# Seven-product MLP kernel: factor splits in two groups, two input sums and all input differences placed amid the first down projection

## The chip, the cores and the metric

One Trainium2 chip, one of its cores. The metric is the device time of one execution in microseconds (us); lower is better. Before the change three runs took 1106.09, 1107.44 and 1108.67 us, median 1107.44 us. Engines are named as in the profile: PE (TensorE matmul, its weight loads PEld), DVE (VectorE), ACT (ScalarE), POOL (GpSimd), SP (SyncE).

## The reference, cut to what matters

A step of a two-layer encoder for 512 prompt tokens and 64 tokens of a running stream (576 columns in all, D = 1024). Layer 0 mixes by pooling, layer 1 by sparse attention; each is followed by the same MLP with a hidden width of 4096:

```python
def _mlp(h, w_up, w_down):
    u = jax.nn.relu(h @ w_up)
    return (u * u) @ w_down
...
        x = x + y.astype(x.dtype)
        x = x + _mlp(_rmsnorm(x, norm_mlp[i]), mlp_w_up[i], mlp_w_down[i]).astype(x.dtype)
```

The change touches only the two MLPs.

## The kernel before, in words

**Layout.** Activations stand transposed: x[k] is a tile of 128 features by 576 tokens, k = 0..7. A float32 product is made of three passes of a reduced type (fp32r): each operand is split into a high part (ACT casts it) and a low part (DVE subtracts the high part from the operand), and the passes are high x high, high x low and low x high. Weight blocks go through the same split in `split_unit` (L182 on ACT makes `wh`, L183 on DVE makes `wl`). Six such units are held at a time, so a weight cast on ACT waits until PE has finished with the unit six places earlier, and DVE's low part waits for the cast.

**Seven products.** `mlp` works in four chunks of 1024 hidden columns. Apart from the up projection of chunk 0 (the plain up: 8 blocks of 48 matmuls in `project`, L306), all is done by `seven` (L497): two by two blocks (two output blocks by the two token halves of 288) are made by seven products instead of eight, 84 matmuls where the plain way takes 96. The price is sums of the inputs. A pair of hidden blocks needs seven factors: b11, b22, b21 as they are and the sums t1, t2, t3, t4. After the plain up `finished` makes them: DVE takes ReLU and scale out of PSUM (L464), ACT squares (L456), DVE forms the sums (`first_sum`, `middle_sums`, `last_sum`, L477 to L484), and `parts_of` splits the factors into `u` (ACT cast L473, DVE subtraction L474). For the first two and the third pair it splits all seven factors in one instruction on each engine, 2016 columns wide. There is one buffer `v` for the unsplit factors of a pair, so that the next pair's L464 waits for the subtraction that reads the last of `v`.

**Sums of x.** The up projections of chunks 1 to 3 are made by `seven` too and need the same of their input: for each of four pairs (x[j], x[j+4]) `x_sums(j)` makes t1, t2, t4 (one ACT activation, three DVE instructions L432 to L434, an ACT cast L435, a DVE subtraction L436), and `x_difference(j)` makes t3 in the place of a quarter of the split input `xs[j]` (DVE L441 and L442, ACT cast L443, DVE L444). The difference overwrites what the plain up reads, so it has to come behind the plain up's matmuls; `x_sums` reads x itself, so it has to come ahead of the down projection that updates those blocks of x in place. Before the change the program has `x_sums(0)` and `x_sums(1)` between the plain ups, `x_sums(2)`, `x_sums(3)` and all four differences at their end, then the four down projections of chunk 0.

**Down.** `Down(q)` with `seven` makes the output blocks x[2q] and x[2q+1]: seven products over the four pairs of the chunk, and six DVE updates of x out of PSUM (L555), some of which must be done before PE may go on in that bank.

**Order.** DMAs are issued by SP (weights) and POOL (sums of weight blocks by accumulating DMA) in the order of a list `jobs`. The order of instructions on each engine is set when the program is built, by a scheduler; it may move an instruction ahead of its place in the code. Each engine then runs its own list strictly in order. Names such as `u_1050` carry a buffer number of the built program; they differ between the two programs.

Of the kernel before, what the change touches and what calls it, by code (L numbers as in the profile page):

```python
# [46 lines left out]
SPARE_UNITS = 6  # L47
RAWS = (4, 3)
MLP_BLOCKS = ("up", "even", "odd", "down")
PLAIN_CHUNKS = 1  # L50
SEEDED = 4
LEAD = 5
UP_ORDER = (0, 4, 1, 5, 2, 6, 3, 7)
FACTORS = ("t3", "t1", "t2", "b11", "b22", "b21", "t4")


@with_exitstack
def pool_dsa_kernel(ctx: ExitStack, tc: tile.TileContext, a, o):
# [13 lines left out]
    def uid(s):  # L72
        count[0] += 1
        return f"{s}_{count[0]}"
# [76 lines left out]
    def mlp_jobs(layer, plain=0):  # L151
        for c in range(4):
            for n, f in enumerate(UP_ORDER):
                kind = "up" if c < PLAIN_CHUNKS else "odd" if n % 2 else "even"
# [127 lines left out]
    def next_block(sub=dve):  # L282
        return [next_unit(5 - i, sub) for i in range(2)]
# [114 lines left out]
    def mlp(layer, gi, late=0, end=None):  # L398
# [22 lines left out]
        def pairs(c):  # L421

            return (KT - LAST if end and c == 3 else KT) // 2

        def x_sums(j):

            t = x_sums_tile()
            xt.append(t)
            raw, first = rough[:, 3 * j:3 * j + 3], rough[:, 12 + j % 2]
            gain, minus = gv[:, gi, j:j + 1], negative[:, half + j:half + j + 1]  # L430
            act.activation(first, x[j][:, :HT], AF.Copy, scale=gain)
            dve.scalar_tensor_tensor(raw[:, 0], x[j][:, HT:], gain, first, ALU.mult, ALU.subtract)  # L432
            dve.scalar_tensor_tensor(raw[:, 1], x[half + j][:, :HT], minus, raw[:, 0], ALU.mult, ALU.subtract)
            dve.scalar_tensor_tensor(raw[:, 2], x[half + j][:, HT:], minus, raw[:, 1], ALU.mult, ALU.subtract)  # L434
            act.copy(t[:, :, 0], raw)  # L435
            dve.tensor_tensor(t[:, :, 1], raw, f32(t[:, :, 0]), ALU.subtract)  # L436

        def x_difference(j):

            b12, b22 = xs[j][:, :, :HT], xs[half + j][:, :, :HT]  # L440
            dve.tensor_tensor(snap, f32(b22), f32(b12), ALU.subtract)  # L441
            dve.tensor_tensor(snap[:, 0], snap[:, 0], snap[:, 1], ALU.add)  # L442
            act.copy(b12[:, 0], snap[:, 0])  # L443
            dve.tensor_tensor(b12[:, 1], snap[:, 0], f32(b12[:, 0]), ALU.subtract)  # L444
# [13 lines left out]
        def activated(pt, v):  # L458

            if isinstance(pt, tuple):  # L460
                for h in range(2):
                    dve.scalar_tensor_tensor(v[:, h], pt[h][:, :HT], 0.0, halves(norm.rb)[:, h], ALU.max, ALU.mult)
            else:
                dve.scalar_tensor_tensor(v, pt[:, :, :HT], 0.0, halves(norm.rb), ALU.max, ALU.mult)  # L464
            square(v)

        def tiles():
            return (phase["acts"].tile([P, 7, HT], F32, tag="v", bufs=1, name=uid("v")),
                    phase["u"].tile([P, 7, 2, HT], F32R, tag="u", bufs=4, name=uid("u")))

        def parts_of(u, v, f):

            act.copy(u[:, f, 0], v[:, f])  # L473
            dve.tensor_tensor(u[:, f, 1], v[:, f], f32(u[:, f, 0]), ALU.subtract)  # L474

        def first_sum(v):
            dve.tensor_tensor(v[:, 1], v[:, 3], v[:, 0], ALU.subtract)  # L477

        def middle_sums(v):
            dve.scalar_tensor_tensor(v[:, 2], v[:, 4], -1.0, v[:, 1], ALU.mult, ALU.subtract)  # L480
            dve.tensor_tensor(v[:, 0], v[:, 4], v[:, 0], ALU.subtract)

        def last_sum(v):
            dve.scalar_tensor_tensor(v[:, 6], v[:, 5], -1.0, v[:, 2], ALU.mult, ALU.subtract)  # L484
# [94 lines left out]
        class Up:  # L579
# [15 lines left out]
                act.copy(snap[:, 1], self.banks[1])  # L595

            def lo0(self):
                self.relu(3, self.banks[0], ALU.max, 1)
                ahead()
                if self.final:  # L600
                    parts_of(self.u, self.v, slice(3, 4))

            def hi1(self):
                v = self.v
                dve.tensor_tensor(v[:, 4], self.banks[1], snap[:, 0], ALU.add)  # L605
                self.relu(4, v[:, 4], ALU.min, 0)
                ahead()

            def hi0(self):
                v = self.v  # L610
                dve.tensor_tensor(v[:, 0], self.banks[2], snap[:, 1], ALU.add)
                self.relu(0, v[:, 0], ALU.max, 0)
                if end and self.at[0] == 3:
                    left_over(self.at[1], v[:, 0])
                parts_of(self.u, v, slice(4 if self.final else 3, 5))
                first_sum(v)
                middle_sums(v)

            def lo1(self):
                v = self.v  # L620
                self.relu(5, self.banks[1], ALU.min, 1)
                if not self.final:
                    ahead()
                parts_of(self.u, v, slice(0, 3))
                last_sum(v)
                if not self.final:
                    ahead()
                parts_of(self.u, v, slice(5, 7))
# [12 lines left out]
        def finished(i, pt, us):  # L641
            nonlocal pair
            if i % 2 == 0:
                pair = tiles()
            v, u = pair
            activated(pt, v[:, 4:6] if i % 2 else v[:, 0:4:3])
            if i == KT - 2:
                first_sum(v)
                for f in (3, 1):
                    parts_of(u, v, slice(f, f + 1))  # L650
            elif i == KT - 1:
                middle_sums(v)
                last_sum(v)
                parts_of(u, v, slice(0, 3, 2))
                parts_of(u, v, slice(4, 7))
# [8 lines left out]
        todo = []  # L664
        snap = None
        for c in range(4):
            us = []
            if c < PLAIN_CHUNKS:
                for i in range(KT):
                    w = next_block()  # L670
                    spreads = c == 0 and i == 2
                    pt = (psum1("up"), psum1("up")) if spreads else psum("up")
                    project(pt, w, xs, spread() if spreads else iter(()))
                    todo.append((i, pt, us))
                    if c == 0 and i < 2:
                        if i:
                            norm.stats()
                        continue
                    for t in todo:
                        finished(*t)  # L680
                    todo.clear()
                    if c == 0 and 3 <= i < 7 and i % 2:
                        x_sums(i // 2 - 1)
# [7 lines left out]
            else:  # L691
                for j in range(half):
                    up = Up(c, j)
                    seven(of_x, False, up)
                    us.append(up.u)
            for q in range(pairs(c)):
                seven(of(us), q == 0, Down(q))
        if end:
            rest = []
            for j in range(half):  # L700
# [857 lines left out]
```

## Time and profile before

| what | value |
|---|---|
| runs shown | 1106.09, 1107.44, 1108.67 us |
| the profiled execution | 1105.9 us, its span 1104.1 us |
| PE busy | 1058.5 us (96%), 7942 matmul records |
| DVE busy | 910.8 us (82%) |
| ACT busy | 628.7 us (57%) |
| granted PE clock, mean | 0.985 |
| plain up of layer 0 / layer 1 | 41 to 96 us / 700 to 755 us |
| down projections of chunk 0 in layer 0 | from 96 us; the first copy of the next up projection (L592) is at 154.7 us |

Times in a row of the timeline are microseconds from the span's start: start, duration, engine, line, operation, output <- input, shape, count, and in brackets the engine's idle time before it and what ended it. PE is busy nearly all the time, so the places where it waits are what can be won. "PEclk" is the share of full clock that PE was granted.

### The profile page before, as it was taken

To read this page: it belongs to the slowest core of one execution; us is meant where nothing else is said; L and a number is where in the kernel's file an instruction comes from. 1 tells how busy PE (TensorE), PEld (TensorE's weight loads), DVE (VectorE), ACT (ScalarE), POOL (GpSimd) and SP (SyncE) were. 2 spreads that over 40 slices of the span, in tenths; PEclk is the share of its full clock that TensorE was granted. 3 is DMA by queue.
4 is the path that set the end of the run, shared out by engine and by line. 5 is a ranking of instruction groups with operands and counts; after the bars stand their busy time and mean duration, and the time that the engine had idled before them with its cause. 6 is when DMAs were issued, how large, how long until landed. Compare 5 with 4: busy or idle time off the path is not lost.

```text
span 1104.1 us, 21662 instructions
## 1 busy us (share of the span) xinstructions
PE 1058.5 (96%) x7942; PEld 1030.0 (93%) x7942; DVE 910.8 (82%) x1837; ACT 628.7 (57%) x1232; POOL 263.4 (24%) x285
## 2 busy tenths in 40 slices
PE   9997999999999999999989999997999999999996
PEld 8997999999999998999979888997999999999895
DVE  7779779879978977779998935679789879978973
ACT  8555357546646745454378776455456547547641
POOL 4100111111111100217687892000111111111101
PEclk9998999999999999999999999998999999999998
DMA  8332666666576564456642454442666676676512
GB/s 248 92 98 74 139 166 164 153 167 160 154 174 163 150 186 134 125 170 173 198 111 66 131 176 117 143 96 67 152 157 164 162 166 162 157 164 163 126 56 86
DMA packets 94459, 157.66 MB, mean 143 GB/s; under 512 B 13729, under 2 KB 25296, under 8 KB 94352
## 3 DMA queue, kind: packets, MB, share of 16 engines
q1 hardware_dynamic: 68720, 109.80, 32.3%
q0 software_dynamic: 15840, 28.84, 16.7%
q10 hardware_dynamic: 9792, 17.63, 5.1%
q8 instruction: 62, 1.02, 0.4%
q14 instruction: 45, 0.37, 0.1%
HBM read 141.15 MB, written 10.89 MB: 138 GB/s over the span
## 4 chain that ended last, share of the span: by engine, by line
PE 80%; DVE 9%; ACT 4%; POOL 2%; issue 2%; DMA 1%; SPq 0%; DVEq 0%; ACTq 0%; POOLq 0%
PE b L497 28%; PE c L497 14%; PE up L306 8%; PE pj L306 7%; PE a L497 7%; PE wo L306 3%; DVE wl L183 2%; PE sc L1255 2%; PE wa L306 1%; PE v L1155 1%; PE pt L1281 1%; PE pb L989 1%; PE dn L306 1%; DVE u L474 1%; ACT wh L182 1%
## 5 line engine op out<-in xcount | busy, mean ns | idle before, releaser
L182 ACT CAST wh<-raw 128x512 fp32r<-128x512 f32 (+1 forms) x316 | 195.3, 620 | 241.2 <-PE b L497 86.1
L183 DVE TENSOR_TENSOR wl<-raw,wh 128x512 fp32r<-128x512 f32 (+1 forms) x294 | 207.7, 708 | 35.8 <-ACT wh L182 29.6
L497 PE MATMUL b<-u,wh 128*128 128x288 f32 x992 | 206.1, 300 | 16.0 <-DVE u L474 6.7
L497 PEld LDWEIGHTS b<-u,wh 128*128 128x128 f32 x992 | 161.5, 191 | 19.9 <-DVE u L474 7.8
L182 ACT CAST wh<-sum 128x512 fp32r<-128x512 f32 x165 | 101.7, 620 | 86.8 <-PE b L497 47.7
L497 PE MATMUL b<-u,wl 128*128 128x288 f32 x496 | 146.8, 298 | 0.0
L183 DVE TENSOR_TENSOR wl<-sum,wh 128x512 fp32r<-128x512 f32 x165 | 112.3, 690 | 34.9 <-ACT wh L182 32.7
L239 POOL DMA_DIRECT2D sum<-in_w_down x31 | 27.1, 891 | 338.0 <-DVE u L474 125.2
L497 PE MATMUL c<-u,wh 128*128 128x288 f32 x496 | 104.5, 298 | 0.1
L497 PEld LDWEIGHTS b<-u,wl 128*128 128x128 f32 x496 | 94.2, 191 | 0.0
L306 PE MATMUL up<-xs,wh 128*128 128x288 f32 x512 | 89.2, 296 | 1.0 <-DVE v L464 1.0
L474 DVE TENSOR_TENSOR u<-v,u 128x576 fp32r<-128x576 f32 (+3 forms) x92 | 81.0, 888 | 6.2 <-ACT u L473 6.2
L497 PE MATMUL b<-xt,wh 128*128 128x288 f32 x384 | 78.1, 296 | 6.8 <-DVE v L605 6.8
L497 PEld LDWEIGHTS c<-u,wh 128*128 128x128 f32 x496 | 80.7, 189 | 1.4 <-DVE x L555 1.2
L497 PE MATMUL b<-xs,wh 128*128 128x288 f32 x384 | 77.2, 295 | 0.0
L306 PEld LDWEIGHTS up<-xs,wh 128*128 128x128 f32 x512 | 74.7, 188 | 1.9 <-DVE v L464 1.4
L473 ACT CAST u<-v 128x576 fp32r<-128x576 f32 (+3 forms) x92 | 71.1, 776 | 8.0 <-DVE v L484 5.8
L497 PE MATMUL c<-u,wl 128*128 128x288 f32 x248 | 73.5, 296 | 0.0
L239 POOL DMA_DIRECT2D sum<-in_w_up x24 | 20.7, 863 | 214.6 <-DVE wl L183 147.8
L497 PEld LDWEIGHTS b<-xt,wh 128*128 128x128 f32 x384 | 61.5, 188 | 8.2 <-DVE v L605 8.2
L306 PE MATMUL pj<-xs,wh 128*128 128x288 f32 x352 | 62.0, 296 | 1.3 <-ACT xs L295 1.3
L497 PEld LDWEIGHTS b<-xs,wh 128*128 128x128 f32 x384 | 61.2, 188 | 0.0
(281 smaller groups left out, 2728.6 us busy)
## 6 DMA issues: line engine op xcount, KB each, us to landing
raw<-in_w_up SPq DMA_DIRECT2D x128, 256.0 KB, 3.0
raw<-in_w_down SPq DMA_DIRECT2D x128, 256.0 KB, 2.8
raw<-in_w_o ACTq DMA_DIRECT2D x32, 256.0 KB, 3.3
sum<-in_w_down SPq DMA_DIRECT2D x31, 256.0 KB, 2.8
sum<-in_w_down POOLq DMA_DIRECT2D x31, 256.0 KB, 4.5
raw<-in_w_down POOLq DMA_DIRECT2D x31, 256.0 KB, 5.0
raw<-in_w_in ACTq DMA_DIRECT2D x30, 256.0 KB, 3.1
sum<-in_w_up SPq DMA_DIRECT2D x24, 256.0 KB, 2.8
```

What stands on the lines that cost most here:

```text
L182: act.copy(h, src)
L183: how["sub"].tensor_tensor(l, src, f32(h), ALU.subtract)
L239: pool.dma_start(s1, odd[:, 512:], accum_op=ALU.add)
L306: pe.matmul(pt[h][:, :m] if isinstance(pt, tuple) else pt[:, h, :m], wt, xs[k][:, part, c:c + m], start=(k == 0 and i == 0), stop=(k == n ...
L473: act.copy(u[:, f, 0], v[:, f])
L474: dve.tensor_tensor(u[:, f, 1], v[:, f], f32(u[:, f, 0]), ALU.subtract)
L497: pe.matmul(bank[:, :HT], wt, ut, start=first and j == 0 and i == 0, stop=j == 3 and i == 2, skip_group_check=True)
L989: pe.matmul(pt[:, c0:c0 + rhs.shape[1]], lhs, rhs, start=n == 0, stop=n == len(steps) - 1)
L1155: pe.matmul(pt[:n, :264], xs[k][:, part, i * P:i * P + n], wt[:, sl], start=(k == 0 and j == 0), stop=(k == KT - 1 and j == 2))
L1255: pe.matmul(pt[:, hh, :nw], q[:, 2 * s + hh], ks[g][:, part, :nw], start=part == 0, stop=part == 1)
L1281: pe.transpose(pp[:, c:c + P], pr[:, hh, kt * P:(kt + 1) * P], ident)
```

## The change

Per MLP: (1) `FACTORS` puts t4 first, so that b11, b22, b21 stand side by side behind the four sums. For the first three pairs of the plain up the split of the seven factors is made in two groups: b11, b22, b21 (864 columns) can be cast while DVE still forms the sums, then the four sums (1152 columns). The last pair's splits are grouped anew too. (2) `x_sums(2)` and `x_sums(3)` move from the end of the plain up behind the first and the second down projection of chunk 0, all differences behind the third. Their scratch is no longer `rough` and `snap` but further uses of the buffer `v`. (3) So that the sums still read x before it is updated, chunk 0 takes its down pairs in the order 0, 2, 1, 3 (pair 0 updates x[0], x[1]; pair 2 x[4], x[5]; `x_sums(2)` reads x[2], x[6] and `x_sums(3)` x[3], x[7]); the list of weight loads follows. Chunks 1 to 3 are the same but for the places of the factors in `u`. No matmul and no DMA is added or taken away: both programs have 7680 matmuls and 427 lines on SP.

```diff
-FACTORS = ("t3", "t1", "t2", "b11", "b22", "b21", "t4")
+FACTORS = ("t4", "t3", "t1", "t2", "b11", "b22", "b21")
+FIRST_DOWN = (0, 2, 1, 3)
...
-            for m in range(KT):
+            for m in range(KT) if c else [2 * q + i for q in FIRST_DOWN for i in range(2)]:
...
-        def x_sums(j):
+        def x_sums(j, raw, first):
...
-            raw, first = rough[:, 3 * j:3 * j + 3], rough[:, 12 + j % 2]
...
             elif i % 2:
+                upper(u, v, slice(4, 7))
                 first_sum(v)
                 middle_sums(v)
                 last_sum(v)
-                parts_of(u, v, slice(0, 7))
+                upper(u, v, slice(0, 4))
+                lower(u, v, slice(4, 7))
+                lower(u, v, slice(0, 4))
...
-                if c == 0:
-                    x_sums(2)
-                    x_sums(3)
-                if c == PLAIN_CHUNKS - 1:
-                    snap = halves(tmp("snap", "s2", 1))
-                    for j in range(half):
-                        x_difference(j)
...
+        def x_prepared(n):
+
+            if n < 2:
+                v = v_tile()
+                x_sums(n + 2, v[:, :3], v[:, 3])
+            elif n == 2:
+                for j in range(half):
+                    if j % 2 == 0:
+                        v = v_tile()
+                    i = j % 2 * 2
+                    x_difference(j, v[:, i:i + 2])
+
+        for n, q in enumerate(FIRST_DOWN):
+            seven(of(us), n == 0, Down(q))
+            x_prepared(n)
```

What the scheduler makes of it is seen in the built programs. First place: DVE in layer 0 at the end of the plain up, where the last pair's factors are made. `xt` are the sums of x, `snap` and `xs` the differences, `u_1050` the third pair's factors, `v_1191` the last pair's, `wl` a weight's low part, `up_1142` and `up_1214` the last two plain up blocks in PSUM. Before:

```order
L436 TENSOR_TENSOR xt_1272<-rough_686,xt_1272 128x3x288
L436 TENSOR_TENSOR xt_1279<-rough_686,xt_1279 128x3x288
L183 TENSOR_TENSOR wl_1321<-raw_918,wh_1320 128x512
L441 TENSOR_TENSOR snap_1286<-xs_657,xs_645 128x576
L474 TENSOR_TENSOR u_1050<-v_1049,u_1050 128x7x288
L183 TENSOR_TENSOR wl_1349<-sum_1130,wh_1348 128x512
L442 TENSOR_TENSOR snap_1286<-snap_1286 128x288
L464 SCALAR_TENSOR_TENSOR v_1191<-up_1142,rbm_149_866 128x2x288
L464 SCALAR_TENSOR_TENSOR v_1191<-up_1214,rbm_149_866 128x576
L444 TENSOR_TENSOR xs_645<-snap_1286,xs_645 128x288
L477 TENSOR_TENSOR v_1191<-v_1191 128x288
```

The same place after the change; the third pair is `u_1054`, the last pair `v_1197`, the last two up blocks `up_1148` and `up_1220`:

```order
L477 TENSOR_TENSOR u_1054<-v_1053,u_1054 128x4x288
L183 TENSOR_TENSOR wl_1211<-raw_914,wh_1210 128x512
L463 SCALAR_TENSOR_TENSOR v_1197<-up_1148,rbm_149_866 128x2x288
L183 TENSOR_TENSOR wl_1299<-raw_920,wh_1298 128x512
L485 TENSOR_TENSOR v_1197<-v_1197 128x288
L477 TENSOR_TENSOR u_1198<-v_1197,u_1198 128x288 x2
L463 SCALAR_TENSOR_TENSOR v_1197<-up_1220,rbm_149_866 128x576
L183 TENSOR_TENSOR wl_1327<-sum_1136,wh_1326 128x512
L488 SCALAR_TENSOR_TENSOR v_1197<-v_1197 128x288
```

The two `xt` and the differences are gone from here; the last pair's first up block is taken out of PSUM, and two of its factors split, ahead of the last up block rather than behind it.

Second place: DVE amid the third down projection of chunk 0 after the change (`x_82` is the tile that it updates, `v_1711` the scratch of the first two differences, `b_1573`, `c_1575`, `a_1574` PSUM banks):

```order
L440 TENSOR_TENSOR v_1711<-xs_654,xs_642 128x576
L440 TENSOR_TENSOR v_1711<-xs_657,xs_645 128x576
L563 TENSOR_TENSOR x_82<-x_82,b_1573 128x288
L183 TENSOR_TENSOR wl_1649<-raw_1414,wh_1648 128x512
L441 TENSOR_TENSOR v_1711<-v_1711 128x288 x2
L563 TENSOR_TENSOR x_82<-x_82,c_1575 128x288
L563 TENSOR_TENSOR x_82<-x_82,a_1574 128x288
L183 TENSOR_TENSOR wl_1668<-sum_1416,wh_1667 128x512
L183 TENSOR_TENSOR wl_1685<-sum_1646,wh_1684 128x512
L443 TENSOR_TENSOR xs_642<-v_1711,xs_642 128x288
L443 TENSOR_TENSOR xs_645<-v_1711,xs_645 128x288
```

Before the change only `wl`, the sums of weight blocks and the updates of x stand there.

More of the change, by code (lines that the diff above doesn't have):

```diff
@@ L153, in mlp_jobs @@
             for n, f in enumerate(UP_ORDER):
-                kind = "up" if c < PLAIN_CHUNKS else "odd" if n % 2 else "even"
+                kind = "odd" if c and n % 2 else "even" if c else "up"
                 jobs.append((kind, a["w_up"][layer, c * 8 + f], KT * P))
-            for m in range(KT):
+            for m in range(KT) if c else [2 * q + i for q in FIRST_DOWN for i in range(2)]:
                 kind = "down" if c == 3 and m >= KT - plain else "odd" if m % 2 else "even"
@@ L436, in x_sums, with x_difference @@
             dve.tensor_tensor(t[:, :, 1], raw, f32(t[:, :, 0]), ALU.subtract)
-        def x_difference(j):
+        def x_difference(j, snap):
             b12, b22 = xs[j][:, :, :HT], xs[half + j][:, :, :HT]
@@ L465, in activated, with v_tile, upper, lower @@
             square(v)
+        def v_tile():
+            return phase["acts"].tile([P, 7, HT], F32, tag="v", bufs=1, name=uid("v"))
         def tiles():
[L468 removed]
+            return (v_tile(),
                     phase["u"].tile([P, 7, 2, HT], F32R, tag="u", bufs=4, name=uid("u")))
+        def upper(u, v, f):
+            act.copy(u[:, f, 0], v[:, f])
+        def lower(u, v, f):
+            dve.tensor_tensor(u[:, f, 1], v[:, f], f32(u[:, f, 0]), ALU.subtract)
         def parts_of(u, v, f):
[L473 to L474 removed]
+            upper(u, v, f)
+            lower(u, v, f)
         def first_sum(v):
[L477 removed]
+            dve.tensor_tensor(v[:, 2], v[:, 4], v[:, 1], ALU.subtract)
         def middle_sums(v):
[L480 to L481 removed]
+            dve.scalar_tensor_tensor(v[:, 3], v[:, 5], -1.0, v[:, 2], ALU.mult, ALU.subtract)
+            dve.tensor_tensor(v[:, 1], v[:, 5], v[:, 1], ALU.subtract)
         def last_sum(v):
[L484 removed]
+            dve.scalar_tensor_tensor(v[:, 0], v[:, 6], -1.0, v[:, 3], ALU.mult, ALU.subtract)
         def left_over(j, b12):
@@ L597, in lo0 @@
             def lo0(self):
-                self.relu(3, self.banks[0], ALU.max, 1)
+                self.relu(4, self.banks[0], ALU.max, 1)
                 ahead()
                 if self.final:
-                    parts_of(self.u, self.v, slice(3, 4))
+                    parts_of(self.u, self.v, slice(4, 5))
             def hi1(self):
                 v = self.v
-                dve.tensor_tensor(v[:, 4], self.banks[1], snap[:, 0], ALU.add)
-                self.relu(4, v[:, 4], ALU.min, 0)
+                dve.tensor_tensor(v[:, 5], self.banks[1], snap[:, 0], ALU.add)
+                self.relu(5, v[:, 5], ALU.min, 0)
                 ahead()
@@ L610, in hi0 @@
                 v = self.v
-                dve.tensor_tensor(v[:, 0], self.banks[2], snap[:, 1], ALU.add)
-                self.relu(0, v[:, 0], ALU.max, 0)
+                dve.tensor_tensor(v[:, 1], self.banks[2], snap[:, 1], ALU.add)
+                self.relu(1, v[:, 1], ALU.max, 0)
                 if end and self.at[0] == 3:
-                    left_over(self.at[1], v[:, 0])
-                parts_of(self.u, v, slice(4 if self.final else 3, 5))
+                    left_over(self.at[1], v[:, 1])
+                parts_of(self.u, v, slice(5 if self.final else 4, 6))
                 first_sum(v)
@@ L620, in lo1 @@
                 v = self.v
-                self.relu(5, self.banks[1], ALU.min, 1)
+                self.relu(6, self.banks[1], ALU.min, 1)
                 if not self.final:
                     ahead()
-                parts_of(self.u, v, slice(0, 3))
+                parts_of(self.u, v, slice(1, 4))
                 last_sum(v)
@@ L627, in lo1 @@
                     ahead()
-                parts_of(self.u, v, slice(5, 7))
+                parts_of(self.u, v, slice(0, 7, 6))
                 if self.final:
@@ new lines, in mlp @@
+        todo, us = [], []
+        for i in range(KT):
+            w = next_block()
+            pt = (psum1("up"), psum1("up")) if i == 2 else psum("up")
+            project(pt, w, xs, spread() if i == 2 else iter(()))
+            todo.append((i, pt, us))
+            if i == 1:
+                norm.stats()
+            if i < 2:
+                continue
+            for t in todo:
+                finished(*t)
+            todo.clear()
+            if i in (3, 5):
+                r = 2 * i - 6
+                x_sums(i // 2 - 1, rough[:, r:r + 3], rough[:, r + 3])
@@ new lines, in mlp @@
+        snap = halves(tmp("snap", "s2", 1))
+        def x_prepared(n):
[11 more added lines that the diff above has]
+            x_prepared(n)
@@ L698, in mlp @@
+        for c in range(1, 4):
+            us = []
+            for j in range(half):
+                up = Up(c, j)
+                seven(of_x, False, up)
+                us.append(up.u)
+            if c < 3:
+                for q in range(half):
+                    seven(of(us), q == 0, Down(q))
+        for q in range(pairs(3)):
+            seven(of(us), q == 0, Down(q))
         if end:
```

39 lines of the change are left out of this document (7 added, 32 removed).

## The prediction

> **What bounds the kernel now.** I read the page first, then the span cut into stages of 10 us, then PE's waits and its timeline in the weakest stages, then DVE's timeline there. Columns of a stage: its length, busy time (instructions) of PE, PEld, DVE, ACT and POOL, PE's granted clock, DMA share, GB/s.
>
> ```profile
> PE 1058.5 (96%) x7942; PEld 1030.0 (93%) x7942; DVE 910.8 (82%) x1837; ACT 628.7 (57%) x1232; POOL 263.4 (24%) x285
> 80.00:90.00 10.00, 10.00 (x79) 10.00 (x78) 10.00 (x21) 5.46 (x9) 0.86 (x1) 1.00 0.28 55
> 90.00:100.00 10.00, 7.12 (x55) 6.89 (x53) 10.00 (x15) 5.56 (x7) 0.00 (x0) 1.00 0.16 52
> 100.00:110.00 10.00, 6.30 (x24) 5.36 (x25) 10.00 (x21) 5.93 (x12) 0.86 (x1) 0.57 0.39 94
> 130.00:140.00 10.00, 10.00 (x77) 10.00 (x76) 8.07 (x15) 3.78 (x7) 1.72 (x2) 1.00 0.71 160
> 150.00:160.00 10.00, 10.00 (x77) 10.00 (x77) 6.75 (x12) 5.07 (x10) 1.72 (x2) 1.00 0.68 170
> 190.00:200.00 10.00, 8.77 (x65) 8.29 (x63) 10.00 (x21) 6.68 (x16) 0.99 (x2) 1.00 0.59 133
> 750.00:760.00 10.00, 7.10 (x52) 6.63 (x50) 10.00 (x15) 5.17 (x7) 0.00 (x0) 1.00 0.16 54
> 760.00:770.00 10.00, 6.47 (x23) 5.75 (x24) 10.00 (x21) 6.71 (x13) 1.73 (x2) 0.51 0.43 106
> ```
>
> PE bounds the kernel, except just behind the plain up of each layer (90 to 110, 750 to 770): there DVE is busy without a break from 80 on, PE waits, and its clock is granted at about half. So DVE bounds that place, and the work that this change takes away stands in it. PE's timeline there, layer 0 and then the two ends of the same stretch in layer 1, and a row of the chain of waits for PE's pace:
>
> ```profile
> 95.80 0.43 PE L306 MATMUL up<-xs,wl 128*128 128x288 f32 x2
> 96.07 0.30 PE L497 MATMUL c<-u,wl 128*128 128x288 f32 x1
> 99.93 0.40 PE L497 MATMUL b<-u,wh 128*128 128x288 f32 x1 [2.88 <-DVE u L474]
> 103.27 0.61 PE L497 MATMUL b<-u,wh 128*128 128x288 f32 x1 [2.54 <-ACT u L473]
> 104.74 0.61 PE L497 MATMUL b<-u,wh 128*128 128x288 f32 x1 [0.53 <-DVE u L474]
> 106.69 0.85 PE L497 MATMUL b<-u,wh 128*128 128x288 f32 x2 [0.62 <-ACT a L526]
> 115.27 0.29 PE L497 MATMUL c<-u,wl 128*128 128x288 f32 x1
> ...
> 755.34 0.29 PE L497 MATMUL c<-u,wl 128*128 128x288 f32 x1
> 774.23 0.29 PE L497 MATMUL c<-u,wl 128*128 128x288 f32 x1
> ...
> 118.90 1.59 PE c L497 x12
> ```
>
> In PE's order 63 matmuls stand between the row at 96.07 and the one at 115.27. At 1.59 us for 12 they need 63 x 0.1325 = 8.35 us; they took 115.27 - 96.07 = 19.20. **Lost: 10.85 us in layer 0, and 18.89 - 8.35 = 10.54 in layer 1, together 21.4 us.** The four waits of layer 0 sum to 6.57 us; the other 4.3 us is the slow clock.
>
> DVE's timeline up to there, and the groups of what the change moves (min/median/max in ns):
>
> ```profile
> 68.06 2.26 DVE L474 TENSOR_TENSOR u<-v,u 128x2016 fp32r<-128x2016 f32 x1 [2.00 <-ACT u L473]
> 78.28 2.26 DVE L474 TENSOR_TENSOR u<-v,u 128x2016 fp32r<-128x2016 f32 x1 [1.09 <-ACT u L473]
> 80.46 0.94 DVE L432 SCALAR_TENSOR_TENSOR rough<-x,gv,rough 128x288 f32<-128x288 f32 x2
> 94.40 2.03 DVE L436 TENSOR_TENSOR xt<-rough,xt 128x864 fp32r<-128x864 f32 x2
> 96.34 0.70 DVE L183 TENSOR_TENSOR wl<-raw,wh 128x512 fp32r<-128x512 f32 x1
> 96.94 0.77 DVE L441 TENSOR_TENSOR snap<-xs,xs 128x576 f32<-128x576 f32 x1
> 97.61 2.27 DVE L474 TENSOR_TENSOR u<-v,u 128x2016 fp32r<-128x2016 f32 x1
> 99.78 0.70 DVE L183 TENSOR_TENSOR wl<-sum,wh 128x512 fp32r<-128x512 f32 x1
> 100.75 1.43 DVE L464 SCALAR_TENSOR_TENSOR v<-up,rbm 128x576 f32<-128x576 f32 x2
> 102.08 0.47 DVE L444 TENSOR_TENSOR xs<-snap,xs 128x288 fp32r<-128x288 f32 x1
> 102.44 0.47 DVE L477 TENSOR_TENSOR v<-v 128x288 f32<-128x288 f32 x1
> 104.21 0.84 DVE L474 TENSOR_TENSOR u<-v,u 128x288 fp32r<-128x288 f32 x2
> ...
> L432 DVE SCALAR_TENSOR_TENSOR rough<-x,gv,rough x8: 510/513/516, 80.5 to 743.7; 128x288 f32<-128x288 f32 x8
> L434 DVE SCALAR_TENSOR_TENSOR rough<-x,negative,rough x8: 515/518/521, 85.6 to 750.2; 128x288 f32<-128x288 f32 x8
> L436 DVE TENSOR_TENSOR xt<-rough,xt x8: 1056/1061/1065, 89.6 to 754.5; 128x864 fp32r<-128x864 f32 x8
> L441 DVE TENSOR_TENSOR snap<-xs,xs x8: 758/764/775, 55.2 to 767.4; 128x576 f32<-128x576 f32 x8
> L442 DVE TENSOR_TENSOR snap<-snap x8: 409/467/477, 56.1 to 769.0; 128x288 f32<-128x288 f32 x8
> L444 DVE TENSOR_TENSOR xs<-snap,xs x8: 460/467/476, 94.0 to 770.4; 128x288 fp32r<-128x288 f32 x8
> ```
>
> The third pair's subtraction (97.61) frees `v`, the last pair is taken out of PSUM only at 100.75, three to four microseconds after PE had ended the plain up, and its first factors are ready at 105. DVE does work in that time that PE needs only 50 us later.
>
> **The change part by part.** Instructions of one stretch follow each other a little faster than they last: 96.34 to 96.94 is 0.60 for a `wl` (and for a weight sum of the same shape), 97.61 to 99.78 is 2.17 for 2016 columns, 0.97 each for the two of 864, 0.66 for an L464, 102.08 to 102.44 is 0.36 for 288 columns, 0.43 for a scalar_tensor_tensor of 288 (0.94 for two). Between 864 and 2016 columns 1152 comes to 0.97 + 1.20 x 288/1152 = 1.27.
>
> *What leaves the place.* A sum of x costs DVE 0.513 + 2 x 0.518 + 1.061 = 2.61 us, a difference 0.764 + 2 x 0.467 = 1.70 us. Two sums and four differences: 5.2 + 6.8 = 12.0 us per layer, of which the first difference's L441 and L442 (1.2 us) had been done at 55; 10.8 us leave DVE's stretch from 80 to 112, the same size as the loss.
>
> *Splits in two groups.* The casts of b11, b22, b21 no longer wait for the sums, so the waits of 2.00 and 1.09 before 68.06 and 78.28 go, at 0.97 + 1.27 - 2.17 = 0.07 us more per split; both together bring DVE forward to the first sum of x at about 77.0 instead of 80.46. I count the extra instructions at nothing: up to 95 DVE now has room.
>
> *The last pair.* In the order of the change, from that first sum of x to the first two factors of the last pair, DVE has 7 `wl`, 2 weight sums (9 x 0.60), 6 x 0.43, 2 x 0.97 for `xt`, 0.97 and 2 x 1.27 for splits, 3 x 0.66, 5 x 0.36 for sums and 2 x 0.36: 17.9 us, against 24.6 before (80.46 to 105.05). From 77.0 that is 94.9. One `wl` among these has to wait for a weight slot (the sixth unit before it is the last up block's first half, which PE ends half a block, 3.2 us, ahead of 95.3), and still leaves time for the rest. PE ends the plain up at 96.07 - 6 x 0.1325 = 95.3, since six matmuls of the down projection that stood ahead of its last block stand behind it now, and comes to the last pair's first factor eight matmuls later, at 96.3: no wait. Behind 95.3 only the last up block's own chain is left (L463, square, three sums, three splits with weight work between, in that order): 6.4 us, until 101.7. PE meanwhile has 22 matmuls of the first two products and 18 for the three finished pairs, until 100.6, and then needs the last pair's b21, whose low part I put at 100.7. A wait of some 0.2 us, too short for the clock.
>
> *What arrives amid the downs.* Four down projections last 4 x 84 x 0.1325 = 44.5 us. DVE's mean share of the rows 130:140 and 150:160 is 74%, 33 us; with 12.0 us more it is 45.0 by durations, and, as 20 instructions follow 0.1 us sooner than they last, 43 by starts: 97%. So DVE is full there but not over-full, and its order is strict: an update of x for which PE waits can stand behind a `wl` that waits for ACT, which waits for PE. Laying the order out with the times above I find four such places per layer (the updates ahead of the third or last product of a down projection, and the one behind the first two `xt`) of 0.3 to 0.6 us, 1.7 us with the first 0.2. The trace of before shows no such wait in these downs; the nearest row, from the up projection that follows, has a single one of 1.14 us:
>
> ```profile
> 196.43 0.53 PE L497 MATMUL b<-xt,wh 128*128 128x288 f32 x2 [1.14 <-DVE v L605]
> ```
>
> The bounds are 0 and, with three waits of that size more, 4 us; I take 1.8 us per layer. ACT (57%) and the down order cost nothing: the loads are the same in number, and SP and POOL have the same kinds of rows in the same order.
>
> **The sum**, against the profiled execution (1105.9): 21.4 - 2 x 1.8 = 17.8, so 1088.1. The median of the runs shown, 1107.44, lies 1.5 above it; half of that added, I say **1089.0**. With all of the loss back it would be 1084.5, with 4 us left per layer 1092.5 (1094.0 on the runs' median).
>
> **The rivals.**
>
> *A wait of 3 us stays and the clock still falls.* Were the last pair's chain longer than I make it, PE would wait once, like the 2.88 at 99.93, and run slowly after: 2.88 + 4.3 = 7.2 us per layer, 21.4 - 14.4 = 7.0 won, 1098.9. For it speaks that the margin at 100.6 is nil, against it that only 0.2 us is missing. The Trainium skill ("TensorE: Matmul & The Clock Gate", Part 1) says that the clock drops to half after an idle window of about 3.4 us; by that a wait of 2.88 alone would leave the clock up, and this case would give 1105.9 - 21.4 + 5.8 = 1090.3. In this trace it is at 0.57 over 100 to 110, after waits of 2.88 and 2.54 with few matmuls between. Chance 0.10.
>
> *The differences come too late for the next up projection.* They end in the middle of the fourth down projection, and the up stage has DVE full (190:200). If the 6.8 us came back as a wait there, 21.4 - 13.6 = 7.8 less 2 for the rest is 6, 1100. Against it: in the order the last difference stands ahead of DVE's last three updates of x, and PE needs it only in the fifth product behind. Chance 0.05.
>
> *DVE's strict order stops the downs: slower.* Each sum and difference waits for an ACT instruction that may stand behind a weight cast waiting for PE, for up to 2.5 us:
>
> ```profile
> ACT wh L182 <- PE b L497: 133.8, 138, 2.5
> ```
>
> Two hops for each sum and one for each difference are eight per layer; beyond 10.7/2.5 = 4.3 of them in full on PE's path the change loses. Seven would give 2 x 17.5 - 21.4 = 13.6 more: 1119.5. Against it: DVE's unfilled quarter in the rows 130:140 and 150:160, and the units held ahead. Chance 0.04.
>
> *It comes out even,* when the same waits take back what is won: 0.02.
>
> **How the numbers follow.** My forecast has 0.79, its own range 1084.5 to 1094.0. The first rival (1098.9) is partly taken in, and the range is 1084.0 to 1098.0. About 0.2% (2.2 us) is what a measurement of this kernel can tell. Faster by more: forecast and the first two rivals, 0.79 + 0.10 + 0.05 = 0.94; within: 0.02; slower: 0.04.
>
> **What would show it.** Right: in the stages 90:100, 100:110, 750:760 and 760:770 PE at 9.5 or more with the clock at 1.00 and no wait for `u` over 1 us; DVE at 9 or more in the stages of the downs; new short waits of PE for x (L563). Wrong: a clock of 0.5 behind the plain up (first rival), waits of several us for `xs` or for L613/L619 in the first up projection (second), PE below 9 in the downs (third).

## The result and the profile after

The changed kernel takes **1087.25 us** (median of four runs, 1086.26 to 1088.53), the kernel before 1106.76 us beside it (1105.42 to 1108.67): ratio 0.9825, 95% interval 0.9811 to 0.9839, 19.5 us less. In two later series it took 1086.96 us against 1105.34 (0.9835, 0.9818 to 0.9853) and 1087.23 against 1105.40 (0.9838, 0.9824 to 0.9852), 18.4 and 18.2 us less. The profiled execution took 1087.99 us, its span is 1086.2 us, its mean granted clock 0.994 (before: 1105.9, 1104.1, 0.985).

The page's line of busy times, then the stages of 10 us of the changed kernel that answer to those shown of before (same columns):

```profile
PE 1050.9 (97%) x7942; PEld 1023.6 (94%) x7942; DVE 909.0 (84%) x1845; ACT 629.3 (58%) x1240; POOL 263.8 (24%) x285
```

```profile
80.00:90.00 10.00, 10.00 (x78) 10.00 (x77) 9.75 (x15) 6.40 (x9) 0.86 (x1) 1.00 0.28 54
90.00:100.00 10.00, 9.83 (x75) 9.59 (x74) 7.22 (x15) 6.33 (x12) 0.01 (x1) 1.00 0.24 80
100.00:110.00 10.00, 10.00 (x77) 10.00 (x77) 9.78 (x19) 5.82 (x10) 1.70 (x2) 1.00 0.63 156
130.00:140.00 10.00, 10.00 (x78) 10.00 (x77) 9.78 (x21) 5.34 (x11) 1.73 (x2) 1.00 0.61 163
750.00:760.00 10.00, 10.00 (x77) 10.00 (x77) 9.77 (x20) 5.99 (x11) 1.74 (x2) 1.00 0.59 144
760.00:770.00 10.00, 10.00 (x77) 10.00 (x76) 9.66 (x19) 4.89 (x9) 1.73 (x2) 1.00 0.65 153
```

The four stages behind the two plain ups (90:110 and 750:770) have PE at 9.83 or more with the clock at 1.00, where before it was 6.3 to 7.1 with a clock down to 0.51. DVE, without a break there before, has 2.8 us free in 90:100 and is full in the stages of the downs (9.78 in 130:140, before 8.07).

PE's timeline of the changed kernel at the end of the plain up of layer 0:

```profile
95.01 0.43 PE L306 MATMUL up<-xs,wl 128*128 128x288 f32 x2
95.27 0.29 PE L505 MATMUL b<-u,wl 128*128 128x288 f32 x1
98.53 0.54 PE L505 MATMUL b<-u,wh 128*128 128x288 f32 x2 [0.17 <-ACT a L534]
105.00 0.29 PE L533 MATMUL a<-u,wh 128*128 128x288 f32 x1
```

70 matmuls stand between the rows at 95.27 and 105.00; at 0.1325 us each they need 9.28 us and took 9.73. The loss here is **0.45 us, where it was 10.85**. In layer 1 the same 70 matmuls take 9.75 us, 0.47 too many, where the loss was 10.54. DVE's timeline shows why: its walk to the last pair's factors.

```profile
73.73 0.94 DVE L431 SCALAR_TENSOR_TENSOR rough<-x,gv,rough 128x288 f32<-128x288 f32 x2
90.13 0.75 DVE L463 SCALAR_TENSOR_TENSOR v<-up,rbm 128x576 f32<-128x576 f32 x1
92.69 0.69 DVE L183 TENSOR_TENSOR wl<-raw,wh 128x512 fp32r<-128x512 f32 x1 [1.81 <-ACT wh L182]
93.74 0.96 DVE L477 TENSOR_TENSOR u<-v,u 128x288 fp32r<-128x288 f32 x2
95.47 0.76 DVE L463 SCALAR_TENSOR_TENSOR v<-up,rbm 128x576 f32<-128x576 f32 x1 [0.77 <-PE up L306]
101.00 0.45 DVE L477 TENSOR_TENSOR u<-v,u 128x288 fp32r<-128x288 f32 x1
```

The last pair's first up block is taken at 90.13, its first two factors are ready at 94.7, 0.6 us ahead of the end of the plain up, and DVE waits twice on the way (1.81 + 0.77 us). Before, the same two factors were ready at 105.

Where the 17.9 us between the two profiled executions came from, by the landmarks in their timelines (first and last matmul of the plain up, first matmul of the next layer's projection `pj`, first of the last projection `dn`). Of the changed kernel, layer 0 to the end:

```profile
41.46 0.77 PE L306 MATMUL up<-xs,wh 128*128 128x288 f32 x4
419.16 0.80 PE L306 MATMUL pj<-xs,wh 128*128 128x288 f32 x4 [1.25 <-ACT xs L295]
745.39 0.42 PE L306 MATMUL up<-xs,wl 128*128 128x288 f32 x2
1053.08 0.29 PE L306 MATMUL dn<-xt,wh 128*128 128x288 f32 x1
```

| kernel (profiled execution) | plain up 0 | rest of MLP 0, to `pj` | `pj` to end of plain up 1 | rest of MLP 1, to `dn` |
|---|---|---|---|---|
| before | 55.11 | 331.69 | 327.59 | 315.44 |
| changed, three executions | 53.98 | 323.72 | 326.65, 324.77, 325.78 | 307.27, 307.28, 307.29 |
| splits only | 54.39 | 328.27 | 326.51 | 311.42 |
| moves only | 54.70 | 325.47 | 326.10 | 309.66 |
| differences moved, sums not | 54.03 | 326.06 | 326.05 | 310.77 |
| sums moved, differences not | 54.40 | 323.53 | 328.31 | 307.21 |
| two differences early, two executions | 54.39 | 322.56, 322.53 | 329.54, 327.11 | 306.62, 306.57 |
| 2.2 us of DVE work put back | 53.99 | 324.06 | 325.53 | 308.25 |
| 6.7 us put back | 53.99 | 328.84 | 327.85 | 312.11 |
| 9.0 us put back | 53.98 | 332.22 | 327.39 | 315.52 |

MLP 0 (its first two columns) won 9.10 us; in layer 1 the last column won 8.17, and part of the 0.94 in the column before it is the six matmuls of the down projection that no longer stand ahead of the plain up's end. The MLP columns repeat to 0.02 us in the three executions of the changed kernel; the stretch between them varies by 1.9. So a difference of half a microsecond in an MLP is read from this table, not from the whole time.

In layer 0, 10.4 of the 10.85 us came back, and the plain up has lost its one wait (0.50 us for L464, at 63.18 before): its column falls by 1.13 us, of which the six matmuls are 0.8. Yet MLP 0 won only 9.10. The rest is given back some 75 us later, in the ups by sevens of chunk 1 and at the start of its downs. PE's waits there in the changed kernel, layer 0 and then layer 1 (the kernel before has one in each layer, of 1.14 and 1.13 us):

```profile
175.12 0.53 PE L505 MATMUL b<-xt,wh 128*128 128x288 f32 x2 [1.32 <-DVE v L613]
187.47 0.53 PE L505 MATMUL b<-xt,wh 128*128 128x288 f32 x2 [0.90 <-DVE v L613]
191.05 0.54 PE L505 MATMUL b<-u,wh 128*128 128x288 f32 x2 [0.28 <-ACT a L534]
...
825.75 0.53 PE L505 MATMUL b<-xt,wh 128*128 128x288 f32 x2 [1.30 <-DVE v L613]
843.05 0.40 PE L505 MATMUL c<-u,wh 128*128 128x288 f32 x1 [0.47 <-DVE u L477]
844.12 0.53 PE L505 MATMUL c<-u,wh 128*128 128x288 f32 x2 [0.28 <-DVE x L563]
```

Together 2.50 us instead of 1.14 in layer 0, 2.05 instead of 1.13 in layer 1. The idle time in brackets is less than what a stop costs, as the 0.17 above with its 0.45 us of loss shows: 10.40 us and the 0.34 won in the plain up, less 9.10, leave 1.64 us given back for 1.36 us more of waits. In the down projections of chunk 0 themselves, from 99 us to their last update of x at about 145, PE waits for nothing.

### The profile page after: what moved, and what is told of

Same layout as the page of the kernel before. It is cut to its first block, busy times and chain, and to the rows that moved or that the text cites. A ratio compares the mean times of both kernels' runs of the same rounds, so it can differ in the third digit from the quotient of the medians.

```text
span 1086.2 us, 21647 instructions
## 1 busy us (share of the span) xinstructions
PE 1050.9 (97%) x7942; PEld 1023.6 (94%) x7942; DVE 909.0 (84%) x1845; ACT 629.3 (58%) x1240; POOL 263.8 (24%) x285
## 4 chain that ended last, share of the span: by engine, by line
PE 75%; DVE 12%; DMA 4%; ACT 3%; issue 3%; POOL 2%; SPq 0%; ACTq 0%; DVEq 0%; POOLq 0%
PE b L505 28%; PE c L505 14%; PE up L306 9%; PE a L505 7%; PE pj L306 3%; DVE wl L183 3%; PE wo L306 3%; DVE work L1231 2%; PE sc L1278 2%; DVE m L1230 2%; PE wa L306 1%; PE pt L1304 1%; PE pb L1012 1%; PE dn L306 1%; DVE u L477 1%
## 5 line engine op out<-in xcount | busy, mean ns | idle before, releaser
L505 PE MATMUL b<-u,wh 128*128 128x288 f32 x992 | 203.2, 296 | 3.4 <-ACT a L534 1.6
L477 DVE TENSOR_TENSOR u<-v,u 128x864 fp32r<-128x864 f32 (+2 forms) x100 | 82.0, 824 | 0.9 <-ACT u L474 0.5
L474 ACT CAST u<-v 128x864 fp32r<-128x864 f32 (+2 forms) x100 | 72.7, 730 | 8.3 <-DVE v L492 5.6
L455 ACT ACTIVATE v<-v 128x288 f32<-128x288 f32 (+1 forms) x112 | 52.1, 476 | 17.2 <-DVE v L596 14.7
```

Of the source, the lines that this page charges most:

```text
L455: act.activation(v, v, AF.Square)
L505: pe.matmul(bank[:, :HT], wt, ut, start=first and j == 0 and i == 0, stop=j == 3 and i == 2, skip_group_check=True)
```

## Experiments

**Splits alone, moves alone.** The first kernel has the new order of `FACTORS` and the splits in two groups, with the sums, the differences and the down order of before; the second has the moves with the splits of before, 2016 columns wide.

Against the changed kernel the first one is:

```diff
-FIRST_DOWN = (0, 2, 1, 3)
+FIRST_DOWN = (0, 1, 2, 3)
...
+        for j in (2, 3):
+            x_sums(j, *old(j))
...
+        for j in range(half):
+            x_difference(j, snap)
...
-            x_prepared(n)
```

Here `old(j)` is the scratch in `rough` that the sums had before.

> Only the new grouping of the factor splits and the new order of the factors; sums and differences of x where they were before, down pairs in the old order. Theory A (the gain comes from the DVE work on x that leaves the end of the plain up): DVE still has the 10.8 us of sums and differences per layer there and is only relieved of its two waits for ACT (2.0 and 1.1 us), so the time falls by at most 2 x 3 us, to 1101 to 1105, with PE's clock still at half behind the plain up. Theory B (the gain comes from the splits no longer waiting, so that the last pair is made earlier): 1088 to 1093, no fall of the clock.

> Only the sums and differences of x moved (and the down pairs in the new order), with the splits of seven factors in one instruction as before. Theory A: most of the gain is here. DVE keeps its two waits (3 us), so the last pair's first factors come at about 98 where PE wants them at 96 to 97: one to three us of waiting per layer, 1089 to 1095, or up to 1100 if the clock falls. Theory B: little changes, 1103 to 1107.

Measured, beside 1106.66 us of before: splits alone 1097.34 us (ratio 0.9917, 0.9891 to 0.9942), moves alone 1091.21 us (0.9859, 0.9838 to 0.9879). The first lies between what the two theories expected and bears out neither; the second is as theory A had it. The gains, 9.3 and 15.5 us, add up to more than the 18.2 to 19.5 of both: each alone shortens the same loss. PE's waits and two stages of the kernel with the splits alone, then the waits with the moves alone:

```profile
99.87 0.40 PE L505 MATMUL b<-u,wh 128*128 128x288 f32 x1 [1.82 <-ACT u L474]
101.34 0.41 PE L505 MATMUL b<-u,wh 128*128 128x288 f32 x1 [0.74 <-DVE u L477]
103.09 0.85 PE L505 MATMUL b<-u,wh 128*128 128x288 f32 x2 [0.74 <-ACT a L534]
...
90.00:100.00 10.00, 8.18 (x62) 7.94 (x61) 10.00 (x17) 5.25 (x10) 0.00 (x0) 1.00 0.27 79
100.00:110.00 10.00, 8.51 (x39) 7.75 (x40) 8.84 (x20) 5.10 (x11) 1.71 (x2) 0.66 0.43 88
```

```profile
98.05 0.40 PE L500 MATMUL b<-u,wh 128*128 128x288 f32 x1 [0.60 <-ACT u L476]
99.24 0.40 PE L500 MATMUL b<-u,wh 128*128 128x288 f32 x1 [0.44 <-DVE u L477]
100.65 0.69 PE L500 MATMUL b<-u,wh 128*128 128x288 f32 x2 [0.51 <-ACT a L529]
...
100.00:110.00 10.00, 9.49 (x61) 9.35 (x60) 8.39 (x16) 5.58 (x10) 1.71 (x2) 0.83 0.45 96
```

With either part alone waits in the same place are left, shorter (3.3 and 1.55 us in sum instead of 6.57), and with them a slow clock.

**Which of the moves.** The whole change, but with the differences at the end of the plain up in `snap`; and the whole change, but with `x_sums(2)` and `x_sums(3)` at their old place in `rough`.

The first, against the changed kernel:

```diff
+        for j in range(half):
+            x_difference(j, snap)
...
-            elif n == 2:
-                for j in range(half):
...
```

The second:

```diff
+        def old(j):
+            return rough[:, 3 * j:3 * j + 3], rough[:, 12 + j % 2]
...
+        for j in (2, 3):
+            x_sums(j, *old(j))
...
-            if n < 2:
-                v = v_tile()
-                x_sums(n + 2, v[:, :3], v[:, 3])
-            elif n == 2:
+            if n == 2:
```

> The whole change, but the four differences stay at the end of the plain up (in the scratch of before). In the built order only one and a half of them stand ahead of the last pair's first factors, the others among its later splits. Theory A: 2 to 4 us of DVE work come back per layer, of which DVE's idle time there (1.8 and 0.8 us after the change) takes the most; 1088 to 1092, clock up. If instead the differences are what mattered: 1095 to 1100.

> The whole change, but the last two sums of x stay at the end of the plain up in the scratch of before, whose buffer the last pair's factors use next; in the built order both sums stand ahead of the last pair. Theory A: 5 us of DVE work per layer come back ahead of the last pair, less some 2.5 us of idle time: PE waits 2 to 3 us per layer and its clock falls or not: 1091 to 1099. If the differences are what mattered: 1087 to 1089.

Measured, beside 1106.66 us and with the splits of the change in both: 1088.53 us (0.9834, 0.9813 to 0.9855) with only the sums moved, 1093.96 us (0.9883, 0.9863 to 0.9903) with only the differences moved. The first cannot be told from the whole change (0.9825 to 0.9838): of the moves, the sums carry the gain. Left at their old place in `rough` they bring back the first wait, 1.43 us, and a clock of 0.80:

```profile
99.05 0.40 PE L505 MATMUL b<-u,wh 128*128 128x288 f32 x1 [1.43 <-ACT u L474]
...
100.00:110.00 10.00, 9.34 (x57) 8.87 (x58) 9.87 (x20) 4.64 (x10) 1.47 (x2) 0.80 0.51 106
```

In that trace the clock reads 0.95 where the others read 1.00, with matmuls at the same 0.1325 us each and a time no longer than that of the kernel's other runs; so 0.80 is to be read against 0.95. The 6.8 us of differences at the end of the plain up cost two waits, 0.48 at 99.08 and 0.74 at 106.61, and no clock:

```profile
100.00:110.00 10.00, 9.26 (x70) 9.02 (x69) 10.00 (x21) 4.90 (x11) 1.71 (x2) 1.00 0.57 112
```

In return the ups of chunk 1 have a single wait of 1.13, and by the table MLP 0 takes 377.93 us with them against 377.70. For where these instructions stand, the built programs show that the place in the code decides nothing here and the scratch does: `rough` is one of the four buffers `u`, and the last pair's factors are its next user, so both last sums have to be through before the last pair is split. Written in `v` tiles at their old place in the code, the sums come out at the same point of DVE's list as in the changed kernel; written in `snap`, the differences come out at the end of the plain up, wherever the code has them. (These two were only built, not timed.)

**The down order alone.** The kernel before with nothing but the pairs of chunk 0 in the order 0, 2, 1, 3.

```diff
+FIRST_DOWN = (0, 2, 1, 3)
...
+            for m in range(KT) if c else [2 * q + i for q in FIRST_DOWN for i in range(2)]:
...
-            for q in range(pairs(c)):
-                seven(of(us), q == 0, Down(q))
+            for n, q in enumerate(range(pairs(c)) if c else FIRST_DOWN):
+                seven(of(us), n == 0, Down(q))
```

> The kernel before with nothing but the down pairs of chunk 0 taken in the order 0, 2, 1, 3, loads alike. Theory A (the order has no price of its own; it only makes room for the sums): 1106.7 us, within 1 us. Theory B (the order itself moves waits, for instance those for x behind the second down projection): over 2 us from it, on either side.

Measured: 1105.97 us beside 1105.34, ratio 1.0005 (0.9993 to 1.0016). The order has no price of its own: theory A.

**Putting DVE work back.** The third pair's two subtractions are written again, with the same values, once, three and four times per layer: 2.24, 6.7 and 9.0 us of DVE work ahead of the last pair's factors.

```diff
                 lower(u, v, slice(4, 7))
                 lower(u, v, slice(0, 4))
+                for _ in range(1 if i == 5 else 0):
+                    lower(u, v, slice(4, 7))
+                    lower(u, v, slice(0, 4))
```

This is the edit of the smallest dose; the others have 3 and 4 in place of the 1.

> The changed kernel with 2.24 us more DVE work ahead of the last pair's factors: the third pair's two subtractions of each layer are written twice (same values). In the trace of the changed kernel DVE has 1.81 + 0.77 = 2.58 us idle there; in the built program the last pair's first factors now stand behind both of its L463, so that they come at about 98.2 instead of 94.2, and PE needs them at 96.3. Theory A (DVE's lateness is a wait of PE one to one, and waits of 2 us behind each other slow the clock): waits of 2 to 2.5 us behind the plain up, clock 0.75 to 0.9 in 100:110, 3 to 4.5 us per layer, 1094.5 us (1091 to 1098). Theory B (the clock does not fall for waits under some 3 us): the waits alone, 1091 us. Theory C (the gain does not hang on when these factors come): 1087 us.

> The changed kernel with three repeats of the third pair's two subtractions in each layer (6.7 us of DVE work; one repeat, 2.24 us, gave waits of 0.51 + 0.88 us per layer, a clock of 1.00 and 1089.2 us, and left 0.51 + 1.43 us of DVE's idle time unused). Two repeats more use that up and push the last pair's factors back by 4.5 - 1.9 = 2.5 us: 3.9 us of waits per layer. Theory A (waits of that size behind each other also slow the clock, as 1.82 + 0.74 + 0.74 us did to 0.66): 1089.2 + 2 x (2.5 + 2) = 1098 us (1096 to 1101), clock 0.6 to 0.85 in 100:110. Theory B (the waits alone): 1089.2 + 2 x 2.5 = 1094 us, clock 1.00.

> The changed kernel with four repeats (9.0 us of DVE work per layer), 2.24 us more than with three: 6.1 us of waits per layer. Theory A (the clock falls as far as in the kernel before, which costs 4.3 us per layer): 1089.2 + 2 x (4.7 + 4.3) = 1107 us (1103 to 1109), clock 0.5 to 0.65 in 100:110: nearly the whole gain gone. Theory B (the waits alone): 1089.2 + 2 x 4.7 = 1098.7 us.

Measured: 1089.18 us (0.9857, 0.9840 to 0.9874) beside 1105.34, and 1099.79 us (0.9941, 0.9924 to 0.9959) and 1104.83 us (0.9988, 0.9978 to 0.9998) beside 1106.09. DVE's and PE's rows and the stage behind with 2.2 us put back:

```profile
92.93 0.69 DVE L183 TENSOR_TENSOR wl<-raw,wh 128x512 fp32r<-128x512 f32 x1 [0.51 <-ACT wh L182]
95.71 0.76 DVE L463 SCALAR_TENSOR_TENSOR v<-up,rbm 128x576 f32<-128x576 f32 x1 [1.43 <-PE up L306]
98.51 0.40 PE L505 MATMUL c<-u,wh 128*128 128x288 f32 x1 [0.51 <-ACT u L474]
100.20 0.40 PE L505 MATMUL c<-u,wh 128*128 128x288 f32 x1 [0.88 <-DVE u L477]
...
100.00:110.00 10.00, 9.80 (x74) 9.80 (x75) 9.89 (x20) 5.53 (x12) 1.71 (x2) 1.00 0.45 93
```

The first dose mostly vanishes in DVE's idle time, and the clock stays at 1.00. The time lies between theories B and C: I had expected the last pair's factors 2 us late for PE, but the scheduler also puts more products of the other pairs ahead of them, and by the table MLP 0 pays 0.35 us and the rest of MLP 1 0.97. Part of that is no effect of the dose at this place: chunk 1 of layer 0 comes out in another order too, with waits of 0.70, 0.66 and 0.26 us, 1.62 instead of 2.50.

Beyond that, theory A holds for the time and the clock of both larger doses. The waits came shorter than I had put them, 2.60 and 4.37 us against 3.9 and 6.1, so more of the loss than I had reckoned is the slow clock. With 6.7 us:

```profile
97.85 0.40 PE L505 MATMUL c<-u,wh 128*128 128x288 f32 x1 [0.64 <-DVE u L477]
100.34 0.40 PE L505 MATMUL b<-u,wh 128*128 128x288 f32 x1 [1.96 <-ACT u L474]
...
100.00:110.00 10.00, 9.50 (x43) 8.44 (x44) 8.95 (x18) 6.50 (x13) 1.50 (x2) 0.66 0.45 89
```

With 9.0 us, DVE's row first:

```profile
100.36 1.42 DVE L463 SCALAR_TENSOR_TENSOR v<-up,rbm 128x576 f32<-128x576 f32 x2
97.71 0.40 PE L505 MATMUL b<-u,wh 128*128 128x288 f32 x1 [0.59 <-DVE u L477]
100.38 0.61 PE L505 MATMUL c<-u,wh 128*128 128x288 f32 x1 [2.13 <-DVE u L477]
102.87 0.61 PE L505 MATMUL b<-u,wh 128*128 128x288 f32 x1 [1.65 <-ACT u L474]
...
100.00:110.00 10.00, 7.84 (x27) 6.58 (x28) 8.88 (x18) 6.02 (x12) 0.63 (x1) 0.50 0.32 61
```

From 2.2 to 9.0 us of work, 6.7 more per layer, the kernel gets 15.65 us slower, 7.8 per layer (by the table 8.15 in MLP 0, 7.27 in the rest of MLP 1): more than one for one, since waits of 4.37 us are followed by a clock of 0.50. DVE then takes the last pair out of PSUM at 100.36, before the change at 100.75, and MLP 0 takes 386.20 us, before the change 386.80.

**The order in chunk 1.** The changed kernel with the differences of pairs 0 and 1 in `snap` behind the plain up; beside it the changed kernel itself, and both once more.

```diff
+        x_difference(0, snap)
+        x_difference(1, snap)
...
             elif n == 2:
-                for j in range(half):
-                    if j % 2 == 0:
-                        v = v_tile()
-                    i = j % 2 * 2
-                    x_difference(j, v[:, i:i + 2])
+                v = v_tile()
+                x_difference(2, v[:, 0:2])
+                x_difference(3, v[:, 2:4])
```

> The whole change, but the differences of pairs 0 and 1 are written behind the plain up with the small tile snap as scratch; those of pairs 2 and 3 stay behind the third down projection in a v tile. In the built program PE takes the products of the first up by sevens in nearly the order that it has before the change (another product stands first), not in the changed kernel's. Theory A (the 1.5 us that the changed kernel loses more per layer in the ups of chunk 1 come from that order of products, which the scratch of the differences sets): one wait of about 1.1 us for L613/L614 per layer there instead of two to three, at most 0.5 us more at the end of the plain up, 2 x 1.3 us less than the changed kernel: 1084.5 us (1083 to 1086). Theory B (those waits come from DVE work being late, whatever the order): the two differences cost about 1 us at the end of the plain up as in the kernel with all four there, and the waits in chunk 1 stay at 2.2 us: 1088 us (1087 to 1089.5).

> The changed kernel itself, beside the kernel that has two differences early, so that both have the same chip and the same runs of the kernel before: 1087.3 us (1086 to 1088.6) by every theory, ratio 0.9825.

> The kernel with two differences early once more, for a second profile of it. From the first pj (the start of the next layer's projections) to the last matmul of the plain up of layer 1 its first profile took 329.1 us, those of the changed kernel 326.2 and 324.4; in the built programs the scheduler has the attention of layer 1 in another order there. Theory A (the other order costs, and takes back what the two MLPs win): 328.5 us or more in that stretch again, the time some 1 us above the changed kernel's. Theory B (that stretch varies by execution): 324 to 327 us in it, and the time 1.4 us below the changed kernel's.

> The changed kernel a third time, beside it: 1087 us; 324 to 326.5 us from the first pj to the last matmul of the plain up of layer 1 by both theories.

Measured: 1088.09 us (0.9846, 0.9829 to 0.9863) and, again, 1086.98 us (0.9839, 0.9822 to 0.9856), the changed kernel beside them 1086.96 and 1087.23: no difference that can be told. PE's waits in layer 0 with two differences early:

```profile
99.16 0.54 PE L505 MATMUL b<-u,wh 128*128 128x288 f32 x2 [0.48 <-ACT a L534]
186.91 0.53 PE L505 MATMUL b<-xt,wh 128*128 128x288 f32 x2 [1.14 <-DVE v L613]
190.49 0.54 PE L505 MATMUL b<-u,wh 128*128 128x288 f32 x2 [0.16 <-ACT a L534]
```

The waits are those that theory A expected: 1.30 us in chunk 1 instead of 2.50, and 0.3 more ahead of it. The plain up has its wait of 0.50 us for L463 again (at 63.44), which the changed kernel does not have. By the table MLP 0 wins 0.75 us (377.70 to 376.95) and the rest of MLP 1 0.65, half of what I had put on it. It is lost in the stretch with the attention of layer 1: 329.5 and 327.1 us against 324.8 to 326.7, of which 0.4 is that wait of 0.50 us in the plain up of layer 1. The scheduler builds the attention in another order there. The 328.5 or more that theory A of the repeat expected did not come back, nor did the 1.4 us below the changed kernel of theory B. Whether that order costs a microsecond or two executions drew a bad lot stays open.

## Why the prediction was right

The forecast was 1089.0 us, with 17.8 us won against the profiled execution; that execution won 17.9, and the median is 1.75 us under the forecast, inside the range. That the two agree to 0.1 us is luck: by medians the gain is 18.2 to 19.5 us, the waits that I placed in the downs came elsewhere (below), and the 0.9 us added for the runs' median had no counterpart, as the changed kernel's median lies 0.7 below its profiled execution.

*The loss behind the plain up* was the right place. Of 10.85 us, 0.45 is left, and putting 9.0 us of DVE work back there, which brings the last pair as late as it was, makes nearly all of it return (ratio 0.9988). That DVE's lateness at the last pair makes the loss is shown by this, not only argued. That the work which left (10.8 us) and the loss were of one size is chance: by the prediction's own count only 24.6 - 17.9 = 6.7 us of it stood ahead of the last pair's first factors, the splits brought the rest, and 4.3 us of the loss was the slow clock. (The last pair was taken out of PSUM 4.5 us behind the end of the plain up, 100.75 against 96.2, not three to four.)

*The splits counted at nothing in instructions, the waits of 2.00 and 1.09 gone*: alone they are worth 9.3 us by the medians, and by the table 4.1 us in MLP 0 and 4.0 in MLP 1, more than the 3.5 us by which I had them bring DVE forward: where PE waits and its clock falls, a microsecond of DVE can be worth more than one.

*The last pair.* DVE's first sum came at 73.73, ahead of the 77.0 that I laid out (it stands between the two groups of the second pair's split now), the two factors at 94.7 instead of 94.9, the end of the chain at 101.45 instead of 101.7. The walk between took 21.0 us instead of 17.9, with that split's second group (1.27) and the wait of 1.81 us for a weight in it; that the earlier start made up for both is luck. The wait of 0.2 us at 100.6 came as 0.17 at 98.53, for ACT's copy of bank b into bank a (L534) rather than for b21.

*The waits amid the downs* are the step that failed. I placed four short waits per layer in the down projections, 1.8 us with the 0.2 at the last pair's b21. There is none in the downs of chunk 0, in either layer: DVE at 9.78 of 10 kept up. (The one wait for x, 0.28 us at 844.12, is in chunk 1.) My reading for it was off as well: of the two rows that I took for the downs, 150:160 lies behind their last update of x (152.67); the rows from 110 to 150 have DVE at 77%, by which my count would have had it at nearly 100% and not 97. The size was right by another cause, and so by luck: the residual of layer 0 is 0.45 us behind the plain up and 1.36 us more of waits in chunk 1, 1.8 together; in layer 1 it is 0.47 and 0.92. These waits go with the order of products that the scheduler builds in chunk 1: in the kernels with the splits alone, only the sums moved and only the differences moved PE has the product order of before in that chunk, and one wait of 1.1 to 1.2 us; with two differences early it has nearly that order, and 1.30 us. The scratch of the sums and differences has a part in that order, but does not decide it alone: the kernel with the moves alone and the three with DVE work put back use the changed kernel's scratch, and have a third pattern, with 1.78 us of waits (0.84, 0.66, 0.28) with the moves alone and 1.6 to 1.7 us with work put back. Why one order waits longer was not tried apart. It is no DVE backlog out of the downs, since DVE has room in the first of those ups, ahead of the waits:

```profile
140.00:150.00 10.00, 10.00 (x78) 10.00 (x78) 7.07 (x13) 4.69 (x10) 1.73 (x2) 1.00 0.64 162
```

*The rivals.* A wait that stays with a slow clock did not come, but the mechanism is real: with 6.7 us of DVE work put back the kernel takes 1099.8 us, where that rival said 1098.9, though with waits of 0.64 and 1.96 us rather than one of 2.88; the changed kernel stands between 2.2 us of DVE work (clock 1.00) and 6.7 (0.66) away from it. The Trainium skill ("TensorE: Matmul & The Clock Gate", Part 1) puts the fall of the clock at an idle window of about 3.4 us; here the longest wait behind a plain up ahead of a slow clock was 2.88 us, and 0.60 + 0.44 + 0.51 us within 3.2 us were followed by 0.83 over ten. Differences too late for the next up: no wait for `xs` and none in the first up; whether the 1.36 us above have to do with them is open. DVE's strict order stopping the downs: no sign.

## What to carry to other kernels

Where an engine is full just ahead of a hand-over and has room behind it, what counts is not its share of busy time but what stands in its list ahead of the instruction that the other engine waits for; here 10.8 us of DVE work per layer moved behind the hand-over, with two of DVE's waits gone ahead of it, won back 10.4 of 10.85 us. What fixes such work in place can be its scratch buffer and not its line in the code: look at who uses the buffer next. A new buffer choice, or a few microseconds more on one engine, also changes the order that a scheduler builds elsewhere, so look for what is given back in the stages behind, and compare those stages rather than whole times when they repeat better.

## What the runs showed of the hardware

The clock answers to waits that are short but close together. Two waits of 0.51 and 0.88 us, 1.7 us apart, left it at 1.00; three of 0.60, 0.44 and 0.51 us within 3.2 us brought 0.83 for the stage 100:110, and in layer 1 0.60, 0.43 and 0.51 brought 0.83 for 750:760; 1.82, 0.74 and 0.74 us brought 0.66, and so did two of 0.64 and 1.96 us; 0.59, 2.13 and 1.65 us brought 0.50. Waits of 0.48 and 0.74 us that were 7.5 us apart cost nothing but themselves: the stage 100:110 kept 1.00. Which of the sum, the number and the spacing of the waits counts, these runs do not separate: 1.39 us in two waits left the clock up, 1.55 us in three did not. Once down, it stayed down behind the last wait: matmuls followed each other in 0.24 us instead of 0.1325 for another 3.6 us with the moves alone (100.65 to 104.3) and for 5.0 us in the kernel before (106.7 to 111.7).
